# A row rotation by DMA: the first 44 blocks' long pieces sent as two halves

## The chip, the cores and the metric

One core of a Trainium2 chip runs the kernel; the other cores are idle. The metric is device time in microseconds (us), the median of three runs. The work is copying: 16 DMA engines belong to the core, and every transfer here runs on them, whoever issues it.

## The reference

```python
x = np.random.randn(8192, 8192).astype(np.float32)
shift = 100
out = np.roll(x, shift, axis=1)
```

Each row of 8192 float32 numbers (32768 B) is rotated right by 100 columns: out[r, 100:] = x[r, :8092] and out[r, :100] = x[r, 8092:]. Nothing is calculated; 268.4 MB are read from the chip's memory (HBM) and 268.4 MB are written to it.

## The kernel before

The output's columns are cut at a = 256 (line 20 rounds 100 up to 128, line 22 adds 128).

**Long pieces** (lines 34 to 43). Columns 256 to 8191 of every row, 7936 numbers or 31744 B, go from HBM to HBM directly: out[r, 256:8192] = x[r, 156:8092]. The 8192 rows are cut into 128 blocks of 64 rows (index c). A block is four DMAs (index j): DMA j holds the 16 rows e*4 + j, e = 0 to 15, and each of the 16 DMA engines gets one of those rows. Even j are issued by SyncE (SP in the profile), odd j by ScalarE (ACT), so each of the two has a queue of its own: q1 and q10 of the profile. A row that goes as one piece is one data packet of 31744 B on one engine, followed by a packet of 4 B that counts the DMA's semaphore up.

For the last four blocks (`c >= blocks - 4`) line 40 makes two parts of the columns, (256, 4224) and (4224, 8192); each is 3968 numbers, 15872 B, and is a DMA of its own on the same queue. So before the change there are 496 DMAs of whole pieces and 32 of halves.

**What orders them.** The framework gives these DMAs eight semaphores, four to each issuing engine, in turn. A DMA waits until the one four places ahead of it on its queue has landed on all 16 engines. So four DMAs per queue, eight in all, can be under way, whatever their size.

**Heads** (lines 60 to 80). Columns 0 to 255 of every row are put together in SBUF. For each of 16 groups of 512 rows, GpSimd (POOL) issues three loads: line 72 brings in pieces of 1024 B that run across the end of one row into the next one, lines 73 and 76 bring short pieces of 400 B and 624 B; VectorE (DVE) copies the long ones into the head tile `h` (lines 74 and 77). When all loads have been issued, POOL issues 16 stores of `h` (line 80). POOL's DMAs go to a third queue, q0, whose packets are 4 KB and less. They have eight semaphores of their own, so here too a later DMA waits for an earlier one.

SP and ACT issue nothing besides the long pieces. No long piece waits for a head or the other way round: the two streams meet only in the 16 DMA engines and in HBM.

Of the kernel before, what the change touches and what calls it, by code (L numbers as in the profile page):

```python
# [1 line left out]

# [4 lines left out]


@with_exitstack
def kernel(  # L10
    ctx: ExitStack,
    tc: tile.TileContext,
    x: bass.AP,
    shift: int,
    out: bass.AP,
):
    nc = tc.nc
    n_rows, n_cols = x.shape
    s = shift % n_cols
    a = -(-s // 128) * 128  # L20
    if 0 < a <= 384 and a + 128 <= n_cols:
        a += 128
    g = a - s
    P = nc.NUM_PARTITIONS
    engines = [nc.sync, nc.scalar]
    n_chunks = 16
    rows = n_rows // n_chunks

    xm = x.rearrange("(c e j) w -> c j e w", e=16, j=4)
    om = out.rearrange("(c e j) w -> c j e w", e=16, j=4)
    if a < n_cols:
        blocks = n_rows // 64
        mid = (a + n_cols) // 256 * 128
        for c in range(blocks):
            parts = ((a, mid), (mid, n_cols)) if c >= blocks - 4 and a < mid else ((a, n_cols),)  # L40
            for j in range(4):
                for lo, hi in parts:
                    engines[j % 2].dma_start(out=om[c, j, :, lo:hi], in_=xm[c, j, :, lo - s:hi - s])
    if a == 0:
        return


    if a > 512:
        for i in range(n_chunks):
            r = slice(i * rows, (i + 1) * rows)  # L50
            nc.gpsimd.dma_start(out=out[r, :s], in_=x[r, n_cols - s:])
            if g > 0:
                nc.gpsimd.dma_start(out=out[r, s:a], in_=x[r, :g])
        return

    Q = 4  # L60
    n_st = n_rows // (P * Q)
    reads = ctx.enter_context(tc.tile_pool(name="reads", bufs=n_st))
    heads = ctx.enter_context(tc.tile_pool(name="heads", bufs=n_st))
    xt = x.rearrange("(k p q) c -> k p q c", q=Q, p=P)
    ot = out.rearrange("(k p q) c -> k p q c", q=Q, p=P)
    tiles = []
    for k in range(n_st):
        t = reads.tile([P, Q - 1, a], x.dtype)
        h = heads.tile([P, Q, a], x.dtype)
        lead = bass.AP(tensor=x.tensor, offset=(k * P * Q + 1) * n_cols - s,  # L70
                       ap=[[Q * n_cols, P], [n_cols, Q - 1], [1, a]])
        nc.gpsimd.dma_start(out=t[:], in_=lead)  # L72
        nc.gpsimd.dma_start(out=h[:, Q - 1, :s], in_=xt[k, :, Q - 1, n_cols - s:])  # L73
        nc.vector.tensor_copy(h[:, :Q - 1, :s], t[:, :, :s])  # L74
        if g > 0:
            nc.gpsimd.dma_start(out=h[:, 0, s:], in_=xt[k, :, 0, :g])  # L76
            nc.vector.tensor_copy(h[:, 1:, s:], t[:, :, s:])  # L77
        tiles.append(h)
    for k, h in enumerate(tiles):
        nc.gpsimd.dma_start(out=ot[k, :, :, :a], in_=h[:])  # L80


# [1 line left out]
_INS = ['x', 'shift']  # L84
_OUTS = [((8192, 8192), 'float32')]

_NUMBERS = {'shift': 100}


# [26 lines left out]
```

## Time and profile before

| | us |
|---|---|
| median of 3 runs | 829.58 (827.68 to 831.9) |
| span of the profiled execution | 828.0 |
| issue of the first long piece (SP, ACT) | 0.75, 0.74 |
| issue of the last long piece on SP and on ACT | 820.3, 822.4 |
| issue of the first and last head store (L80) | 242.2, 379.6 |
| head store, issue to landing, median | 108.2 |
| SP's 88th whole piece, the last of block 43, issued | 281.8 |
| one issue on SP, on ACT | 0.510, 0.517 |

The page of the profile gives, for each DMA queue, its packets, the bytes moved, and the time that its packets took as a share of 16 engines' time. A byte of a long piece is counted once there, but is read from HBM and written to it; a byte of q0 crosses HBM once, since its other end is SBUF. The share of a stretch can stand a little over 1.00, since a packet is counted whole where it starts.

Of the engines, VectorE is busy for 12.3 us and POOL for 41.3 us of the span; the DMAs are everything else.

### The profile page before, as it was taken

The numbers are of one execution on the slowest core, as the hardware profiler recorded it, in microseconds if no ns is written. First come the engines' busy times: TensorE is split into PE (matmuls) and PEld (weight loads), VectorE is DVE, ScalarE is ACT, GpSimd is POOL, SyncE is SP. The second block draws the span as 40 slices with busy tenths as digits, with TensorE's granted clock in tenths as the row PEclk, the third lists the DMA queues.
The fourth block names the chain that finished last, engine by engine and source line by source line (L and its number), as shares of the span: only waits on it lengthen the run. The fifth ranks groups of instructions, "written<-read, shape, count | busy, mean of one in ns | idle before, by whom it ended". The sixth has DMA issues, their size and how long they took to land. (4 is left out here: it accounts for less than half of the span.)

```text
span 828.0 us, 689 instructions
## 1 busy us (share of the span) xinstructions
DVE 12.3 (1%) x32; POOL 41.3 (5%) x68
## 2 busy tenths in 40 slices
DVE  0000000000010000000000000000000000000000
POOL 2011000000021100000000000000000000000000
DMA  9999999999999999999999999999999999999998
GB/s 308 340 350 334 344 340 337 337 339 344 337 342 348 352 351 345 354 339 346 347 341 344 333 325 325 319 330 333 330 324 322 335 330 328 322 331 328 327 314 300
DMA packets 22278, 276.90 MB, mean 334 GB/s; under 512 B 9473, under 2 KB 9729, under 8 KB 13825
## 3 DMA queue, kind: packets, MB, share of 16 engines
q1 hardware_dynamic: 8448, 130.04, 46.1%
q10 hardware_dynamic: 8448, 130.04, 44.7%
q0 software_dynamic: 5376, 16.78, 8.4%
q14 instruction: 6, 0.04, 0.0%
HBM read 268.44 MB, written 268.44 MB: 648 GB/s over the span
## 5 line engine op out<-in xcount | busy, mean ns | idle before, releaser
L80 POOL DMA_DIRECT2D out_dram<-h x16 | 11.5, 724 | 126.6 <-DMA out_dram<-h 86.8
L76 POOL DMA_DIRECT2D h<-in_x_dram x16 | 8.7, 542 | 141.4 <-DMA t<-in_x_dram 141.4
L72 POOL DMA_DIRECT2D t<-in_x_dram x16 | 12.2, 762 | 30.8 <-DMA h<-in_x_dram 30.0
L73 POOL DMA_DIRECT2D h<-in_x_dram x16 | 8.9, 559 | 39.9 <-DMA h<-in_x_dram 39.9
L74 DVE COPY h<-t 128x300 f32<-128x300 f32 x16 | 6.1, 382 | 260.2 <-DMA t<-in_x_dram 260.2
L77 DVE COPY h<-t 128x468 f32<-128x468 f32 x16 | 7.5, 467 | 0.0
L97 POOL MEMSET const-float32-0.0<- 128x1 f32 x1 | 0.1, 99 | 0.2 <-issue 0.2
L97 POOL MEMSET const-bfloat16-1.0<- 128x1 bf16 x1 | 0.1, 102 | 0.0
L97 POOL MEMSET const-float32-1.0<- 128x1 f32 x1 | 0.1, 99 | 0.0
L97 POOL MEMSET const-uint8-127<- 128x1 uint8 x1 | 0.1, 99 | 0.0
## 6 DMA issues: line engine op xcount, KB each, us to landing
out_dram<-in_x_dram ACTq DMA_DIRECT2D x248, 496.0 KB, 12.7
out_dram<-in_x_dram SPq DMA_DIRECT2D x248, 496.0 KB, 12.7
out_dram<-h POOLq DMA_DIRECT2D x16, 512.0 KB, 108.2
t<-in_x_dram POOLq DMA_DIRECT2D x16, 384.0 KB, 50.6
out_dram<-in_x_dram SPq DMA_DIRECT2D x16, 248.0 KB, 6.0
out_dram<-in_x_dram ACTq DMA_DIRECT2D x16, 248.0 KB, 5.9
h<-in_x_dram POOLq DMA_DIRECT2D x16, 78.0 KB, 43.2
h<-in_x_dram POOLq DMA_DIRECT2D x16, 50.0 KB, 49.9
```

The lines of the kernel that those rows point to most:

```text
L72: nc.gpsimd.dma_start(out=t[:], in_=lead)
L73: nc.gpsimd.dma_start(out=h[:, Q - 1, :s], in_=xt[k, :, Q - 1, n_cols - s:])
L74: nc.vector.tensor_copy(h[:, :Q - 1, :s], t[:, :, :s])
L76: nc.gpsimd.dma_start(out=h[:, 0, s:], in_=xt[k, :, 0, :g])
L77: nc.vector.tensor_copy(h[:, 1:, s:], t[:, :, s:])
L80: nc.gpsimd.dma_start(out=ot[k, :, :, :a], in_=h[:])
L97: nc = _bacc.Bacc("TRN2", target_bir_lowering=False, num_devices=1)
```

## The change

One condition: for c below 44, too, the long piece of a row is cut into the two parts, so that each of these blocks is eight DMAs of 16 pieces of 15872 B and not four DMAs of 16 pieces of 31744 B. The halves of one j are issued one after the other on the same queue. 176 DMAs of whole pieces become 352 of halves; blocks 44 to 123 stay whole and the last four stay halved. The bytes, the columns at which rows are cut, the heads and the number of semaphores are what they were.

```diff
         for c in range(blocks):
-            parts = ((a, mid), (mid, n_cols)) if c >= blocks - 4 and a < mid else ((a, n_cols),)
+            parts = ((a, mid), (mid, n_cols)) if (c < 44 or c >= blocks - 4) and a < mid else ((a, n_cols),)
             for j in range(4):
                 for lo, hi in parts:
                     engines[j % 2].dma_start(out=om[c, j, :, lo:hi], in_=xm[c, j, :, lo - s:hi - s])
```

## Prediction

> **What bounds the kernel now.** I read the page's counts first, then the DMA queues, then stretches of the span, and last what SP's queue waits for. The chain of waits I put aside: it ends with POOL's last head store, issued at 379.6 us, and most of its tail is "another core or an unknown queue", so it does not follow the queues of SP and ACT, which run to the end.
>
> ```profile
> span 828.0 us, 689 instructions
> DMA  9999999999999999999999999999999999999998
> q1 hardware_dynamic: 8448, 130.04, 46.1%
> q10 hardware_dynamic: 8448, 130.04, 44.7%
> q0 software_dynamic: 5376, 16.78, 8.4%
> HBM read 268.44 MB, written 268.44 MB: 648 GB/s over the span
> ```
>
> The 16 DMA engines are occupied from the first slice to the last: the three queues' shares add to 99.2%. Nothing is won by filling idle engines. But being occupied is not the same as being fast, so the next view is the stretches (us, busy times of DVE and POOL, clock, DMA share, GB/s). In the order of the rows: loads of the heads beside whole pieces, stores of the heads beside whole pieces, whole pieces alone, the switch to halves at the end, halves alone.
>
> ```profile
> 20.00:250.00 230.00, 10.00 (x26) 25.44 (x41) 1.00 1.00 340
> 300.00:460.00 160.00, 0.00 (x0) 4.29 (x6) 1.00 1.01 346
> 500.00:780.00 280.00, 0.00 (x0) 0.00 (x0) 1.00 0.99 328
> 795.00:805.00 10.00, 0.00 (x0) 0.00 (x0) 1.00 0.93 303
> 805.00:824.00 19.00, 0.00 (x0) 0.00 (x0) 1.00 0.95 330
> ```
>
> To compare them I need HBM traffic, in which a long piece counts twice and a byte of q0 once. For that, the queues of the first and second stretch:
>
> ```profile
> q10 hardware_dynamic: 2220, 35.37, 42.0%
> q1 hardware_dynamic: 2240, 35.49, 40.1%
> q0 software_dynamic: 2717, 7.42, 17.4%
> ...
> q1 hardware_dynamic: 1556, 24.73, 46.9%
> q10 hardware_dynamic: 1557, 24.76, 43.7%
> q0 software_dynamic: 1628, 5.91, 10.2%
> ```
>
> First stretch: 2 x (35.37 + 35.49) + 7.42 = 149.1 MB in 230 us, 648 GB/s. Second: 2 x 49.49 + 5.91 = 104.9 MB in 160 us, 656. Whole pieces alone: 2 x 328 = 656. The switch: 2 x 303 = 606. Halves alone: 2 x 330 = 660. The mix of transfers changes a great deal, the HBM traffic hardly. So I take the bound to be the copying rate through HBM, near 650 GB/s, and not a queue, a wait or an issue.
>
> Durations say the same. In the packet records of the trace a whole piece takes 1.173 us at the least, but among whole pieces alone the mean is 99.3% x 280 us x 16 engines / (5785 packets / 2 data packets) = 1.54 us: a quarter of it is stalling, which expands until the rate is met. For the halves of 805 to 824 us it is 95.4% x 19 x 16 / (792 / 2) = 0.73 us against a least of 0.589.
>
> Last, SP's waits and the two sizes' landings:
>
> ```profile
> SPq L43 <- DMA out_dram<-in_x_dram: 680.3, 260, 4.9
> ...
> out_dram<-in_x_dram SPq DMA_DIRECT2D x248, 496.0 KB, 12.7
> out_dram<-h POOLq DMA_DIRECT2D x16, 512.0 KB, 108.2
> t<-in_x_dram POOLq DMA_DIRECT2D x16, 384.0 KB, 50.6
> out_dram<-in_x_dram SPq DMA_DIRECT2D x16, 248.0 KB, 6.0
> ```
>
> SP waits before 260 of its 264 issues: the four-deep window always binds. A half lands in 6.0 us and a whole piece in 12.7, so landing goes with the bytes ahead in the window, with no fixed part to be seen.
>
> **The change part by part.** *Issues.* 176 more DMAs, 88 on SP and 88 on ACT, at 0.51 us: 45 us on each sequencer. They sit inside SP's 680 us of waiting: in the stage a queue would issue a half every 281.8 / 176 = 1.6 us, three times the 0.51 us needed. Cost 0. Without that cover it would be 45 us.
>
> *Packets.* Block by block each engine had one whole piece per DMA: 44 x 4 = 176. They become 352 halves and 176 more 4 B packets. By the least durations of the packet records, 2 x 589 + 9 - 1173 = 14 ns each, 176 x 14 = 2.5 us per engine. Where the memory is the limit this only takes the place of stalling, cost 0; where the engine is, 2.5 us. I take the middle, 1.2 us, as both are near: share 1.00 and HBM at its usual rate.
>
> *The heads move forward.* An engine appears to take packets from its queues by turns: in the stretch of stores q1, q10 and q0 have 1556, 1557 and 1628 packets. So q0 gets about one turn for every packet of q1, and a half's packets come twice as often. Per engine q0 has 5376 / 16 = 336 packets in all; q1 had 88 DMAs x 2 packets = 176 in the first 44 blocks and would have 352. The head traffic, whose last packet now starts at 490.6 us, could be nearly over when block 43 is. Loads' landings (50.6 us) and stores' (108.2 us) shrink towards half. POOL issues 48 loads and 16 stores as before; its waits of 141.4, 86.8, 39.9 and 30.0 us shrink, and nothing behind them ends the span. What is late next is nothing: q1 and q10 have 80 whole blocks to go. Worth 0 directly.
>
> *The rate in the stage.* This is the only large term. Traffic of the first 44 blocks: 44 x 64 rows x 31744 B = 89.4 MB, twice, plus all 16.8 MB of q0: 195.6 MB. At the 648 GB/s of the stretch of loads, 302 us, as now. Halves beside the heads occur nowhere in the trace, so I bound them by the two rows of halves: at 660 it is 296 us, 5 us less; over 795 to 824 together, 2 x (3.03 + 6.27) MB in 29 us = 641, it is 305 us, 3 us more; at the 606 of the switch alone, 323 us, 21 us more. I take 648, since the heads are there as in the stretch of loads, and it lies between 641 and 660. Term 0.
>
> *A rule against it.* The Trainium skill, "DMA: Bandwidth & Descriptors", section "Rules for kernel authors", asks for 1 MiB or more per DMA and for coalescing, and the fit of its section "Anatomy of one DMA — SWDGE (gpsimd) path" gives each DMA of POOL about 2.0 us besides its bytes. By that, 176 x 2.0 us spread over eight under way would be about 44 us more, an estimate from that page. The landings above disagree: 6.0 against 12.7 leaves no fixed part. The sum keeps 0.
>
> *Sum.* 0 + 1.2 + 0 + 0 = 1.2 us. Against the profile's own span: 828.0 + 1.2 = 829.2. The median of the runs lies 1.6 us above that span, so I forecast 829.6 + 1.2 = 830.8, **831 us**, no change that can be told: 0.5%, about what a measurement of this kernel can tell from none, is 4.1 us.
>
> **The rivals.** *The engines run dry (slower).* The window counts DMAs, so halves leave half the bytes under way. When one engine lags, the others run to the end of the window sooner and stand idle until the slow one has landed. For: the share is 0.93 and 0.95 in the rows of halves, 0.99 to 1.01 elsewhere; the heads' uneven packets add to the spread. Against: at share 0.95 the halves still reached 330 GB/s, because the memory served the rest faster, and q0's packets fill gaps. Price where the memory doesn't make it up: 302 / 0.95 = 318 us, +16 us, 846 us. It decides once the stage's HBM traffic falls under about 638 GB/s (195.6 / 638 = 306.6 us, +5).
>
> *The heads out of the way (faster).* Halves at their own 660 rather than 648 in the stage: -5 us, and from then on whole pieces alone at 656. For: the stretch of loads is the slowest of the long ones. Against: 656 to 648 is worth only 230 x 8 / 656 = 2.8 us, and the stretch of halves is 19 us short. 829.6 - 5.3 = 824 us.
>
> *The heads don't move.* POOL's loads form a chain of waits; if that chain and not the turn sets q0's pace, q0 ends near 490 us still. The time is then 830 us, inside my forecast.
>
> **How the numbers follow.** Forecast (with the last rival) 0.40, its own range 825.5 to 833.7. Dry engines 0.35, since the direction of that row is plain and only the memory's slack holds it off; 834 to 851, with 846 as worked out. Heads out of the way 0.25, 820 to 825. The range that leaves out about 2 in 10 is 821 to 847; the 606 row (851) and anything better than 660 are outside. Faster 0.25, same 0.40, slower 0.35.
>
> **What would show it.** Right: HBM traffic over the first 290 us between 641 and 660, DMA share there 0.96 or more, halves landing in 6 to 8 us, q0's last packet well before 400 us, stretches after that at 656. Dry engines: share under 0.95 before block 44, fewer than 641 GB/s. Heads don't move: last head store issued near 380 still. The prediction is wrong if halves beside q0 stall for longer than halves alone did, or if HBM gives more than 660 to shorter pieces; neither has a row here.

## The result and the profile after

The changed kernel takes 831.55 us (median of 14 runs, 829.4 to 834.52) against 828.35 us for the kernel before (14 runs, 826.85 to 831.9). The ratio is 1.0035, 95% interval 1.0025 to 1.0046: some 2.9 us (2.1 to 3.8) slower, inside the 0.5% that the prediction called no change, yet clear of zero. The two medians themselves stand 3.2 us apart. The profiled execution's span is 830.2 us, 2.2 us longer than the one before.

The page of the profile after: span, DMA share in slices and queues, then the issues with KB each and microseconds to landing.

```profile
span 830.2 us, 865 instructions
DMA  9999999999999999999999999999999999999998
q1 hardware_dynamic: 11264, 130.05, 47.2%
q10 hardware_dynamic: 11264, 130.05, 45.5%
q0 software_dynamic: 5376, 16.78, 6.1%
HBM read 268.44 MB, written 268.44 MB: 647 GB/s over the span
...
out_dram<-in_x_dram SPq DMA_DIRECT2D x160, 496.0 KB, 12.5
out_dram<-in_x_dram ACTq DMA_DIRECT2D x160, 496.0 KB, 12.5
out_dram<-in_x_dram SPq DMA_DIRECT2D x192, 248.0 KB, 6.6
out_dram<-in_x_dram ACTq DMA_DIRECT2D x192, 248.0 KB, 6.5
out_dram<-h POOLq DMA_DIRECT2D x16, 512.0 KB, 28.4
t<-in_x_dram POOLq DMA_DIRECT2D x16, 384.0 KB, 14.5
```

The engines are as occupied as before (shares adding to 98.8%). Halves land in 6.5 us, half of a whole piece's time. The surprise is in the heads: a load lands in 14.5 us instead of 50.6, a store in 28.4 instead of 108.2. That is 3.5 and 3.8 times as quick, not twice. In the packet records q0's last packet starts at 156.8 us, where it was 490.6.

The same execution in stretches (us, DVE and POOL busy, clock, DMA share, GB/s): heads beside halves, their end, halves alone, whole pieces alone, halves alone at the end.

```profile
20.00:150.00 130.00, 10.53 (x28) 33.04 (x52) 1.00 1.01 376
150.00:160.00 10.00, 0.00 (x0) 0.00 (x0) 1.00 0.88 301
160.00:290.00 130.00, 0.00 (x0) 0.00 (x0) 1.00 0.99 326
340.00:780.00 440.00, 0.00 (x0) 0.00 (x0) 1.00 0.99 327
805.00:824.00 19.00, 0.00 (x0) 0.00 (x0) 1.00 0.95 328
```

376 GB/s, where the kernel before had 341, looks like a gain. It is none: q0's bytes cross HBM once, not twice. The queues from 20 to 150 us, first after, then before:

```profile
q0 software_dynamic: 4841, 15.24, 34.8%
q1 hardware_dynamic: 2144, 16.97, 34.3%
q10 hardware_dynamic: 2107, 16.67, 31.7%
```

```profile
q10 hardware_dynamic: 1245, 19.91, 41.4%
q1 hardware_dynamic: 1260, 19.94, 40.0%
q0 software_dynamic: 1629, 4.46, 18.2%
```

HBM traffic, long pieces counted twice: after 2 x 33.64 + 15.24 = 82.5 MB, before 2 x 39.85 + 4.46 = 84.2 MB. The changed kernel falls behind by 1.6 MB here, at 650 GB/s about 2.5 us. As the heads end (150 to 160 us) the share drops to 0.88 and 598 GB/s cross HBM, another 0.8 us. From 160 to 290 us it has 84.9 MB against 84.4 and wins back 0.7 us. Afterwards whole pieces go at 2 x 327, against 2 x 328. Counted from the start, the changed kernel is 2.7 MB behind at 160 us (4.1 us at 650 GB/s), 2.2 MB at 290, 0.6 MB at 500, when the kernel before has finished its heads too, and 1.1 MB at 780. So in these two executions the loss arises in the first 160 us, and most of it is won back by 500 us; the rest comes late, between programs that do the same there, and is no larger than the differences among executions of the kernel before (826.85 to 831.9 us). Whether short pieces or the crowd of heads beside them made it, two profiles can't tell: the experiments were made for that.

### The profile page after: what moved, and what is told of

Its sections match the earlier page's. It is cut to its first block, busy times and chain, and to the rows that moved or that the text cites. A ratio compares the mean times of both kernels' runs of the same rounds, so it can differ in the third digit from the quotient of the medians.

```text
span 830.2 us, 865 instructions
## 1 busy us (share of the span) xinstructions
DVE 12.0 (1%) x32; POOL 41.3 (5%) x68
## 6 DMA issues: line engine op xcount, KB each, us to landing
out_dram<-h POOLq DMA_DIRECT2D x16, 512.0 KB, 28.4
t<-in_x_dram POOLq DMA_DIRECT2D x16, 384.0 KB, 14.5
```

## Experiments

Two theories for the 2.9 us. *Crowding*: the heads, squeezed into 157 us, keep the engines on packets that use one side of HBM only. *Halving*: shorter pieces cost something wherever they run. All ratios below the first are to the kernel before timed beside them on the same chip; its medians there were 826.55, 826.21 and 826.20 us on three chips. Together:

| run | last packet of the heads, us | ratio | 95% interval |
|---|---|---|---|
| the kernel before | 490.6 | 1 | |
| the change | 156.8 | 1.0035 | 1.0025 to 1.0046 |
| halves_late | 528.6 | 1.0022 | 1.0010 to 1.0033 |
| halves_22 | 153.3 | 1.0027 | 1.0010 to 1.0044 |
| halves_all | 163.1 | 1.0050 | 1.0032 to 1.0068 |
| nohead_whole | none | 0.9664 | 0.9648 to 0.9680 |
| nohead_halves | none | 0.9684 | 0.9671 to 0.9698 |
| nohead_halves_all | none | 0.9718 | 0.9700 to 0.9737 |
| halves_paired | 375.7 | 1.0023 | 1.0011 to 1.0036 |
| quarters_44 | 79.9 | 1.0945 | 1.0927 to 1.0964 |
| quarters_full | 247.5 | 1.0084 | 1.0064 to 1.0104 |
| wholes_paired | 737.4 | 1.0101 | 1.0083 to 1.0120 |
| wholes_paired_84 | 689.1 | 1.0072 | 1.0055 to 1.0088 |
| queues_swapped | 478.2 | 1.0009 | 0.9998 to 1.0020 |

**A control.** How far does an edit that should cost nothing move this kernel? It exchanges the two issuing engines (the arguments, left out here, stay):

```diff
-                    engines[j % 2].dma_start(...)
+                    engines[1 - j % 2].dma_start(...)
```

> The kernel before with SP's and ACT's long pieces exchanged: no theory has a cost for it. A control of how far a neutral edit moves the time here: ratio 0.999 to 1.001. If it lands at 1.002, differences of 0.2% between programs mean nothing and only crowding plus the 0.35% of the change are left to explain.

1.0009 with an interval that holds 1 and reaches 1.0020. So 0.1% is about the floor here. The ratios of 1.0022 and 1.0023 below have intervals that overlap this one: by itself, neither can be told from an edit that should cost nothing.

**The heads taken out.** Both kernels return after the long pieces, so they leave out columns 0 to 255 of the output.

```diff
-    if a == 0:
-        return
+    return
```

> Leaves out columns 0 to 255 (no loads, copies or stores of heads); long pieces as in the kernel before. It is the base for the next run. Both theories: the heads carry 16.8 MB of HBM traffic, at 655 GB/s 25.6 us, so about 803 us; ratio to the kernel before 0.969.

> Leaves out columns 0 to 255; long pieces of the first 44 blocks in halves, as in the changed kernel. Theory 1, crowding (the 2.9 us come from the heads being squeezed into the first 157 us beside the halves, where the engines and not HBM set the rate): without heads there is nothing to crowd, within 0.7 us of the run with whole pieces and no heads. Theory 2, halving itself (packets, short window, wherever halves run): 2.5 to 3.5 us over the run with whole pieces and no heads.

The medians are 799.12 and 800.48 us: 1.4 us between them, between the two forecasts, and the intervals overlap. The first run missed its own forecast: without heads it was 27.8 us faster (26.4 to 29.1), not 25.6, so the heads cost more than their bytes at 655 GB/s. Taken further, with every block in halves:

```diff
-            parts = ((a, mid), (mid, n_cols)) if c >= blocks - 4 and a < mid else ((a, n_cols),)
+            parts = ((a, mid), (mid, n_cols)) if a < mid else ((a, n_cols),)
```

> Leaves out columns 0 to 255; all 128 blocks in halves, a DMA each. The own cost of halving at its largest, with no heads to crowd: 124 / 44 x 1.4 us (what 44 blocks cost without heads) = 3.9 us over whole pieces without heads, ratio to the kernel before 0.969 to 0.973. If halving has no cost of its own and only crowding has, 0.9655 to 0.968.

0.9718 against 0.9664, each to the kernel before on its own chip, and here the intervals are apart: 0.0054 x 826 = 4.5 us for 124 blocks more in halves, with no heads anywhere (about 2.5 to 6.5, from the two intervals). Halving has a cost of its own, about 0.036 us a block; 44 blocks make 1.6 us (0.9 to 2.3), an estimate by the number of blocks.

**Halves elsewhere.** Only the condition of line 40 is shown, before and then for halves_late, halves_22 and halves_all in this order:

```diff
-  if c >= blocks - 4 and a < mid
+  if 80 <= c and a < mid
+  if (c < 22 or c >= blocks - 4) and a < mid
+  if c >= 0 and a < mid
```

> Blocks 0 to 79 whole, 80 to 127 in halves: 44 blocks of halves more than the kernel before, as in the changed kernel, but after the heads are done. Theory 1, crowding: the heads run as in the kernel before, time within 0.7 us of it (ratio 0.999 to 1.001). Theory 2, halving itself: the same 2.5 to 3.5 us as the changed kernel, ratio 1.003 to 1.004.

> Halves only in blocks 0 to 21 and the last four. In the changed kernel the heads were done at 157 us, which is about when block 23 is issued, so nearly all heads still run beside halves. Theory 1, crowding: nearly the whole cost, 2.2 to 3.0 us, ratio 1.0027 to 1.0036. Theory 2, halving itself: half of the cost, 1.2 to 1.7 us, ratio 1.0015 to 1.002.

> All 128 blocks in halves, a DMA each. Both theories: the own cost of halving, 1.6 us for 44 blocks, grows with their number to 124 / 44 x 1.6 = 4.5 us, and the crowding of the heads adds its 1.3 us: 5 to 7 us, ratio 1.006 to 1.0085. If the cost were tied to a change of size within a queue and not to the halves, it would be under 3 us.

Neither theory takes all. With 44 more blocks halved where hardly any heads are left beside them, 0.22% or 1.8 us stay: between the two forecasts, under that of halving and over that of crowding. With 22 blocks, 0.27% or 2.2 us (0.8 to 3.6), as crowding says, though the interval still holds the 0.8 us of 22 halved blocks. With all blocks, 0.50% or 4.1 us, under the forecast of both, where 4.5 for halving alone leave nothing for the crowd. The own cost is clear of noise once, in the runs without heads that halve every block or none; the other figures agree with it. A crowding cost of some 1.3 us is suggested by the change, by halves_22 and by the first 160 us of the trace, and the intervals are too wide to call it shown.

The other traces carry it a little further. HBM traffic from 20 to 150 us, reckoned as above, is 635, 643 and 641 GB/s in the change, halves_22 and halves_all, whose heads end near 157 us. It is 645 to 651 in the kernel before, queues_swapped, halves_late, halves_paired, wholes_paired and quarters_full, whose heads end at 247 us or later, and 649 to 654 in the three runs without heads. A rate lower by 1% is 1.3 us in 130 us, the size that is looked for; each figure comes from one execution.

In the trace of halves_late, the stretch that has whole pieces and the heads' stores, and the one that has halves alone, read:

```profile
300.00:520.00 220.00, 0.00 (x0) 5.70 (x8) 1.00 1.01 343
...
550.00:780.00 230.00, 0.00 (x0) 0.00 (x0) 1.00 1.00 326
```

Halves alone: 2 x 326 = 652 GB/s, as in the changed kernel from 160 to 290 us. Whole pieces alone had 2 x 328 = 656 before. 0.6% of the 300 us that 44 blocks take is 1.8 us, the size of the own cost. But the view rounds to 1 in 327, and in the runs without heads it reads 326 for whole pieces and 326 for halves from 20 to 290 us, 328 and 327 from 290 to 780. The rate agrees with such a cost and does not prove it.

**Is it the window or the piece?** A window of eight DMAs holds half as many bytes when the DMAs are halves. The next run keeps pieces of 15872 B but puts two rows of an engine in each DMA, so that the window holds what it held before.

```diff
+            if c < 44:
+                for j in (0, 2):
+                    for i, (lo, hi) in enumerate(((a, mid), (mid, n_cols))):
+                        engines[i].dma_start(
+                            out=om[c, j:j + 2, :, lo:hi].rearrange("j e w -> e j w"),
+                            in_=xm[c, j:j + 2, :, lo - s:hi - s].rearrange("j e w -> e j w"))
+                continue
```

> First 44 blocks in halves, but two rows per engine in a DMA: left halves of rows j and j + 1 on SP, right halves on ACT. Pieces are 15872 B as in the changed kernel, DMAs are as many and as large as in the kernel before, so the window holds the bytes it held before. Theory W (the halves cost because the window of eight DMAs holds half the bytes and queues run dry, which also lets q0 in): heads end at 300 to 400 us, not at 157, and the time is within 1 us of the kernel before, ratio 0.999 to 1.001. Theory P (short pieces cost whatever the window, and by their turns let q0 in): heads end near 160 to 200 us, 2 to 3 us slower, ratio 1.0025 to 1.0035.

Theory W was right on the heads, which end at 375.7 us. On the time it missed its range: 1.0023 (1.0011 to 1.0036), where theory P has it, though not apart from the control either. Its page:

```profile
out_dram<-in_x_dram SPq DMA_DIRECT2D x248, 496.0 KB, 12.7
out_dram<-h POOLq DMA_DIRECT2D x16, 512.0 KB, 73.4
t<-in_x_dram POOLq DMA_DIRECT2D x16, 384.0 KB, 35.2
```

With the same pieces but a full window the heads take 375.7 us, not 157. So it was not the shorter turns alone that tripled the heads' pace. Counting packets separates the two. When the last of q0's 336 packets per engine starts, q1 has started 297 per engine in the kernel before, 311 in halves_paired, 339 in wholes_paired and 348 in quarters_full: about one for one, as the prediction's turn says, wherever the window is full (290 to 348 in all such runs with heads). In the changed kernel it has started 161, and in quarters_44, the next run, 110: q0 gets two and three packets to a turn. With half the bytes under way, it seems, an engine's two long queues are empty now and then, and q0 is served alone until the next long piece comes. The queues of the changed kernel from 105.3 to 107.2 us show such a moment:

```profile
q0 software_dynamic: 185, 0.67, 91.5%
q1 hardware_dynamic: 11, 0.06, 8.3%
q10 hardware_dynamic: 10, 0.05, 6.0%
```

q0 holds nine tenths of the engines, and 2 x 0.11 + 0.67 = 0.89 MB cross HBM in 1.9 us, about 470 GB/s instead of 650. This is what the crowding theory means. The time of halves_paired, though, is still 1.9 us over the kernel before (0.9 to 3.0), with the window full.

The window shows most in the next run: quarters, a DMA each.

```diff
+            if c < 44:
+                parts = tuple((a + 1984 * i, a + 1984 * (i + 1)) for i in range(4))
```

> First 44 blocks in quarters of 7936 B, a DMA each. Theory P: three further pieces a row where the changed kernel has one, so three times its own cost of 1.6 us and the crowding of 1.3: about 6 us, ratio 1.006 to 1.009. Theory W: eight quarters are 8 x 0.37 = 3.0 us of work for an engine, less than the 4.7 us that the quickest half took to land, so once the heads are done the queues are dry for a third of the time: 20 us or more, ratio above 1.02.

It is 78 us slower, as theory W had it (20 us or more). From 150 to 340 us of its trace, when the heads are done (DMA queues and issues):

```profile
DMA packets 12059, 47.89 MB, mean 252 GB/s; under 512 B 6028, under 2 KB 6028, under 8 KB 12057
...
q1 hardware_dynamic: 6033, 23.93, 41.2%
q10 hardware_dynamic: 6024, 23.94, 38.9%
...
out_dram<-in_x_dram SPq DMA_DIRECT2D x189, 124.0 KB, 4.0
out_dram<-in_x_dram ACTq DMA_DIRECT2D x189, 124.0 KB, 4.0
```

The engines are occupied for 80% of the stretch, and the rate is the window over the landing: 8 x 126976 B / 4.0 us = 254 GB/s, measured 252. The changed kernel has, for whole pieces from 340 to 780 us and for halves from 160 to 290 us:

```profile
out_dram<-in_x_dram SPq DMA_DIRECT2D x141, 496.0 KB, 12.4
...
out_dram<-in_x_dram ACTq DMA_DIRECT2D x84, 248.0 KB, 6.2
```

8 x 507904 B / 12.4 us = 328, and 8 x 253952 B / 6.2 us = 328, obey the same equation, but the other way round: with the engines busy throughout, the rate is given and the landing follows from it. The quarters' landing did not halve once more: it went from 6.2 to 4.0 us (3.1 to 4.7 in this stretch) with the engines idle a fifth of the time, and there the rate follows the landing. What a quarter waits for in the rest of its 4.0 us, no run separates.

Quarters with a full window, four rows of an engine in one DMA:

```diff
+            if c < blocks - 4:
+                for i in range(4):
+                    lo, hi = a + 1984 * i, a + 1984 * (i + 1)
+                    engines[i % 2].dma_start(
+                        out=om[c, :, :, lo:hi].rearrange("j e w -> e j w"),
+                        in_=xm[c, :, :, lo - s:hi - s].rearrange("j e w -> e j w"))
+                continue
```

> Blocks 0 to 123 in quarters of 7936 B, but four rows per engine in a DMA: DMAs are as many and as large as in the kernel before, so the window holds the bytes it held. Theory W, the window alone costs: within 2 us of the kernel before, ratio 0.998 to 1.0025, where quarters of a DMA each cost 78 us in 44 blocks. Theory P, short pieces cost: 4 x 0.298 - 1.173 = 0.019 us for each of 496 rows per engine at the least, 9 us, ratio 1.008 to 1.013.

7.0 us in 124 blocks instead of 78 us in 44: the window, a quarter full there, made nearly all of the loss of quarters. What remains fits theory P: 1488 further pieces per engine, 4.7 ns each, against 19 / 3 = 6.3 ns by the least durations. But several rows in a DMA may have a price too, as the last pair suggests.

**The opposite edit**: whole pieces, two rows of an engine in a DMA, twice the bytes under way; below is wholes_paired, and wholes_paired_84 has `c < 84` for its condition.

```diff
+            if c < blocks - 4:
+                for i in range(2):
+                    engines[i].dma_start(
+                        out=om[c, 2 * i:2 * i + 2, :, a:].rearrange("j e w -> e j w"),
+                        in_=xm[c, 2 * i:2 * i + 2, :, a - s:n_cols - s].rearrange("j e w -> e j w"))
+                continue
```

> Blocks 0 to 123: whole pieces, two rows per engine in a DMA (992 KB), half as many DMAs, a window of twice the bytes; last four blocks as before. Theory W: engines run dry less than in the kernel before, 1 to 3 us faster, ratio 0.996 to 0.999. Theory P: pieces are as before, so within 0.7 us, ratio 0.999 to 1.001.

> Whole pieces two rows per engine and DMA in blocks 0 to 83, one row from there on, the last four blocks as before. Theory E (the 8 us of the run with all blocks paired come from its end: engines that had spread over a window of 25 us fall in step again only in the last 30 us, where the DMA share was 0.65 to 0.85): nearly all of it goes, ratio 0.999 to 1.003. Theory H (slower heads or large DMAs cost wherever they are): two thirds of it stay, ratio 1.005 to 1.008.

Both theories of wholes_paired failed: it is 8.3 us slower. The stretches of wholes_paired:

```profile
480.00:740.00 260.00, 0.00 (x0) 4.28 (x6) 1.00 1.00 334
740.00:790.00 50.00, 0.00 (x0) 0.00 (x0) 1.00 1.00 328
...
800.00:810.00 10.00, 0.00 (x0) 0.00 (x0) 1.00 0.65 252
```

Heads run until 737 us, and the switch to halves near the end has a share of 0.65 where the kernel before had 0.92. The end was the first suspect. wholes_paired_84, whose last 40 blocks before the halves are as in the kernel before, still loses 5.9 us, two thirds and a little more of it, as theory H said. So the end holds the smaller part. Whether the rest is the slower heads, the order in which rows reach HBM, the doubled window, or DMAs of two rows, was not separated. With it, the 1.9 us of halves_paired and the 7.0 us of quarters_full can't be put down to short pieces alone.

No version that writes the whole output was faster than the kernel before.

## The prediction, step by step

**The number: right, in part by luck.** 831 was forecast and 831.55 measured. But the sum started from 829.6, the median of three runs, and 14 runs have 828.35; and it put the change at 1.2 us, where it is 2.9. The two errors, 1.3 too much and 1.7 too little, nearly cancel.

**The bound: right.** HBM traffic stayed between 635 and 654 GB/s in the changed kernel's three stretches of 130 us and more, however the queues shared it, and the time moved by 0.35%. The signs named for being right were there: 642 GB/s from 20 to 290 us (638 if the first 20 us are counted in), a share of 1.00, halves landing in 6.6 us, the heads' end at 156.8 us, and 654 after that.

**Issues at nothing: right.** SP issued 88 more DMAs and its waiting fell by 45 us, from 680.3 to the following, as the step had it:

```profile
SPq L43 <- DMA out_dram<-in_x_dram: 635.2, 344, 4.2
```

**Packets at 1.2 us, from 0 to 2.5: right in size, the kind open.** Halving's own cost is 1.4 to 1.8 us for 44 blocks: 1.8 in halves_late, 1.4 without heads, 1.6 from all blocks without heads. That is 8 to 10 ns for each of the 176 extra pieces per engine, under the 14 ns of the least durations. That these nanoseconds are what costs is argued, not shown: halves, a DMA each, also halve the bytes under way, and halves_paired, which has them in full, packs two rows into a DMA.

**The heads at twice the pace: mis-sized.** The step counted turns and had them nearly over when block 43 is, around 290 us. They were over at 157 us. By the step's turns they would have been over near 290 x 336 / 352 = 277 us, and the packet counts bear the turns out where the window is full. The step left out that q0 also gets what an empty long queue leaves, though the rival of dry engines, further on, said that queues would be empty. halves_paired, where they are not, gives 376 us; it also has fewer packets on q1, one of 4 B for two halves.

**The rate in the stage at 648: mis-sized, and with it the sum.** From 20 to 290 us the queues of the changed kernel carried

```profile
q1 hardware_dynamic: 5005, 39.69, 43.0%
q10 hardware_dynamic: 4959, 39.36, 39.8%
q0 software_dynamic: 4855, 15.28, 16.8%
```

2 x 79.05 + 15.28 = 173.4 MB in 270 us, 642 GB/s, just above the lower of the two bounds, 641. By the step's own division 195.6 / 642 = 304.7 us instead of 302: 3 us, which holds the packets' cost too. The sum had 1.2 us and 2.9 were measured. (The step's "302 us, as now" is loose: from 20 to 290 us the kernel before moved only 9.41 of the 16.8 MB of heads. It prices the same bytes on both sides, so the difference stands.) The upper bound, 660, came from 19 us of halves at the end of the kernel; over 130 us halves alone reach 653.

**The rivals.** The dry engines named the right mechanism, long queues that run empty, and priced it by engines that stand idle. They did not: in the stage q0 took the free engines, and the share stayed at 1.01 until the heads ended, fell to 0.88 for 10 us, and was 0.99 from then on. The rival's 16 us belong to shorter pieces: quarters lost 78. The heads out of the way gave back 0.7 us from 160 to 290 and 2.4 us more up to 500 (137.9 MB against 136.4), and had cost more than that before. "The heads don't move" was wrong.

**A rule against it.** The estimate from the Trainium skill ("DMA: Bandwidth & Descriptors"), about 44 us, was 15 times the 2.9 us measured, and DMAs of 992 KB, near the size that its section "Rules for kernel authors" asks for, were 1.0% slower than those of 496 KB. The page's fit is for POOL's DMAs, though, and its row for transfers of 128 partitions; these are HBM to HBM from SP and ACT. What decided between halves and quarters was bytes under way over landing time.

## What to carry to other kernels

Before cutting DMAs smaller under a fixed number in flight, divide the bytes that the window will hold by a short landing of the trace at hand (here 4.7 us, the quickest half of the kernel before). Halves give 8 x 253952 B / 4.7 us = 432 GB/s, well above the present 328, and the cut cost little; quarters give 216, below it, and ran at 252. These two sizes are all that was tried. Where the memory sets the rate, letting one stream go ahead sooner buys nothing unless something waits for it. And GB/s of a queue view rises when transfers that cross HBM once move forward: count the crossings before calling it a gain.

## What the runs showed of the hardware

A queue of small packets is slowed by the long packets beside it far more than by its own bytes. q0's packets are of 4 B to 4368 B in every run (256 of them a little over 4 KB). With every head DMA unchanged, the heads ended at 80 us beside quarters, 157 beside halves, 376 beside halves with a full window, 491 beside whole pieces and 737 beside pairs of them.

With a window of twice the bytes the engines drift further apart: in the semaphore records a DMA's first engine landed about 16 us before its last (SP's queue, mean, 20 to 250 us), where it was 6.7 us with whole pieces of a row and 2.2 us with halves. In halves_paired, halves with a full window, it was 6.7 us too, so it goes with the bytes under way and not with the length of a piece. That the switch to small DMAs at the end has to pay such drift back is a reading of the share of 0.65 there, not shown by itself.
